# A hybrid decoder step on one core: rows gathered in their own order, early up weights in halves, the new tokens' residual in quarters

## The chip, the cores and the metric

The kernel runs on one core of one Trainium2 chip. The metric is device time in microseconds of one launch; a time that is compared is a median over several runs. One further execution was recorded by the hardware profiler, and every duration below comes from that one.

The engines are named as in the profile: PE (matmuls) with PEld (its weight loads), DVE (vector), ACT (scalar), POOL (GpSimd) and SP, whose queue issues nearly all loads of weights. Each engine works through its own instructions in their order and waits at semaphores.

## The reference

One step of one decoder layer in fp32, for 256 prompt tokens and 8 new tokens (one each for 8 sequences with 1024 past tokens in a paged cache):

```python
xn = rmsnorm(x, g_mix);  q, k, v, b, c, h = split(xn @ w_in)      # 1024 -> 6 x 512
att  = moba_attend(rope(q), [past k, rope(k)], [past v, v])      # top-3 blocks of 256 and the own block
conv = b * short_conv(c * h)
hres = x + concat(att, conv) @ w_out                             # the residual
hn   = rmsnorm(hres, g_ffn)
# router: group = argmax of 4, then the top 2 of that group's 8 experts, in fp32
h = silu(hn @ w_gate[e]) * (hn @ w_up[e]) * gate[e]              # 32 experts, 1024 -> 256
y = hres + sum_e h @ w_down[e];   y = rmsnorm(y, g_final)
```

Only the experts that a token chose count for it, so the kernel sends to each expert just its own tokens, 32 places each. The weights of the 32 experts are 96 MiB and are each read once.

## The kernel before, in words

**Tokens.** `yres[128, 3, 1024]` is the residual: t=0 and t=1 are the prompt's tokens, t=2 holds the 8 new tokens in partitions 0 to 7. `NR` = (128, 128, 8) are the tokens of each t.

**First stage.** Everything up to the router is cut into named steps, and the string `ORDER` says in which order they are issued; each engine keeps that order among its own instructions. Those that matter here: `o{t}{n}{kk}` the output projection (L779) and its add to `yres`, with `o111` and `o112` the two halves of the last; `z{n}` the output projection of the new tokens, made as four partial products that lie in the four quarters of 32 partitions, and `y{n}` the sum of these quarters (`sum_quarters`, L268) and its add to `yres` (`out_sum`, L800: four adds on 8 partitions for each half of 512 columns); `H{t}{k}` the square sum, transposes (`pt`) and scaled copy `xh` of the residual; `l{t}{k}` the router's matmuls (L878); `R`, `L`, `ra` to `re` the norm's factor and the routing of each t on DVE; `rk` and `oh` the rank of a token among its expert's and the one-hot map `Pg` from tokens to places; `hl0` the split of a residual into `hn` (rounded to fp32r, L853) and `hlo` (what is left, L868).

**Gathering.** For a group of four experts, `gather_mm` multiplies the one-hot map with the residual rows (`px`, in two halves `hf` of 512 columns), `gather_rows` copies `px` out of PSUM to `xr`, and `gather_T` transposes `xr` into `xg`, the stationary operand of the experts' matmuls. Group 0 uses `yres` itself in fp32 (L1035; each such matmul is two records of the profile), groups 1 to 7 use `hn` and `hlo` in fp32r. The expert weights lie in memory so that partition p of a weight tile holds rows 8p to 8p+7, so column 8p+c of a token has to come to partition p of chunk c. Before the change this reordering is done where `px` reads its moving operand (every eighth column for group 0) and where `hn` and `hlo` are written. In `ORDER` the gather of group 0 is `g{t}{hf}`, `ga{hf}` and `gt{hf}`.

**Experts.** A loop over eight groups `grp`: the gate matmuls `pgt` (`mm_exp`, L1205; the first matmul of each of the four experts waits for its weights), the combination of the group before (`combine_all`: `pz`, L1236, and six adds to `yres`), maps and gate values, the up matmuls `pup`, the product `sh`, its transposes `pht`, the gather of the next group, the down matmuls `pyy` (L1219) and their scaling to `Y` (`gated`). In the last group, `LAST` = 7, come also the matmuls that start the final sum from `yres` (`before`, `pzl`, L1247) and twelve matmuls that only keep PE occupied (`warm`), and the down weights and the end are cut into pieces.

**Buffers and loads.** A pool has a number of equal buffers, and a new tile takes one that is released; what first writes the tile waits for the last reader of the one before. `c4` has 10 buffers of 4 KB a partition (`xn`, `qT`, `kT`, `vn`, `kn`, `uT`, `pn`, `pT`, `Pp`, `xh`, `xr`, `xg`, `hn`, `hlo`, `Y`, and the halves `uh`), `c2` has 9 of 2 KB (among them `yq`, `Pg` and the quarters `uq`). Weights of the experts go round a ring of 15 slots of 1 MiB: two `c9`, nine `rk` (which held the cache's keys and values) and four `rw` (which held input and output projection weights). SP issues, in this order: `g0` (four gate tiles of group 0), `d0`, `g10` and `g11`, then the up weights of group 0, which have no slot of the ring but `c4` and `c2` buffers (experts 0, 1, 3 in two halves each, expert 2 in four quarters), then `g12`, `g13`, `u1`, `d1` and so on. With 15 slots, `u13` and `d10` to `d12` take the slots of `g0`, and `d13` and `g20` to `g22` those of `d0`. For group 7 the up weights come in halves and the down weights in twelve pieces.

Of the kernel before, what the change touches and what calls it, by code (L numbers as in the profile page):

```python
# [11 lines left out]
F32 = mybir.dt.float32  # L12
# [4 lines left out]
OP = mybir.AluOpType  # L17
# [24 lines left out]
cv2 b3 B10 b2 V3 cv0 V0 c2 c3 ov V2 V1 B13 eB1 G25 o010 kvs pe0 o000 eB3 G26 eB0 G27 G28 G29 o110 G30 V5 eB2 V4  # L42
o001 V6 H00 G31 o011 V7 H01 l00 pa pe o100 R0 l01 L0 ra0 rb0 rc0 o101 as co room1 rd0 re0 z0 z1 rk0 oh0 y0
y1 H10 H20 H21 l20 R2 l21 L2 ra2 rb2 room2 o111 rc2 rd2 l10 o112 H11 R1p H12a R1 H12b rk2 oh2 l11 l12 L1 ra1 rb1 rc1
g00 g01 rsa g20 rk1p rk1 oh1 g21 g10 ga0 g11 gt0 ga1 rsb gt1 rd1 sl re2 re1 hl0
"""


C_ROPE, C_SEL, C_IOTA, C_W4, C_W8, C_WT, C_HEAD, C_TOK, C_W = 0, 96, 104, 136, 140, 148, 152, 160, 172


def _table():
    t = np.zeros((128, C_W), np.float32)
    p = np.arange(128)
    inv = np.float32(500000.0) ** (-np.arange(0, 16, 2, dtype=np.float32) / np.float32(16))
    for i in range(3):
        pos = (p + 128 * i if i < 2 else np.full(128, 1024)).astype(np.float32)
        ang = pos[:, None] * inv[None, :].astype(np.float32)
        c, s = np.cos(ang), np.sin(ang)
        t[:, C_ROPE + 32 * i:C_ROPE + 32 * i + 32] = np.concatenate([c, c, -s, s], 1)  # L60
    t[:, C_SEL:C_SEL + 8] = (p[:, None] % 32) == np.arange(8)
# [27 lines left out]
def hymba_step(ctx: ExitStack, tc: tile.TileContext, x_prompt, x_sample, cache_k, cache_v, state_conv,  # L89
# [35 lines left out]
    with tc.manual_schedule():  # L125
# [139 lines left out]
        def sum_quarters(acc, x):  # L265

            for j in range(4):
                T.matmul(acc[32 * j:32 * j + 8, 0:128], lhsT=sel8, rhs=x[:, 128 * j:128 * j + 128], start=True, stop=True,  # L268
                         tile_position=(0, 32 * j))

# [524 lines left out]
        def out_sum(n):  # L795
            po2 = ps("py2", "acc")
            sum_quarters(po2, yq[n])
            for j in range(4):
                yv = yres[0:8, 2, 512 * n + 128 * j:512 * n + 128 * j + 128]
                V.tensor_tensor(yv, yv, po2[32 * j:32 * j + 8, 0:128], op=OP.add)  # L800

# [43 lines left out]
        def norm2_hi(t, a, w):  # L845
            n, p = NR[t], slice(a // 8, (a + w) // 8)
            if a == 0:
                hn[t] = c4(f"hn{t}", [128, 8, 128], F32R)
# [4 lines left out]
            S.copy(hn[t][:n, :, p].rearrange("t c p -> t p c"),  # L853
                   yres[:n, t, a:a + w].rearrange("t (p c) -> t p c", c=8))

# [7 lines left out]
        def norm2_lo(t, a, w):  # L863

            n, p = NR[t], slice(a // 8, (a + w) // 8)
            if t not in hlo:
                hlo[t] = c4(f"hlo{t}", [128, 8, 128], F32R)
            V.tensor_tensor(  # L868
                hlo[t][:n, :, p], yres[:n, t, a:a + w].rearrange("t (p c) -> t c p", c=8),
                hn[t][:n, :, p].bitcast(F32), op=OP.subtract)  # L870

# [155 lines left out]
        def gather_mm(grp, hf, tiles):  # L1027
# [5 lines left out]
            for t in tiles:  # L1033
                if grp == 0:
                    T.matmul(PX[grp, hf], lhsT=fl(PgS[grp], t, 128).bitcast(F32),  # L1035
                             rhs=yres[:, t, :].rearrange("t (p c) -> t c p", c=8)[:, 4 * hf:4 * hf + 4, :],
                             start=t == first, stop=t == last)
                    continue
                n = 40 if t == 2 else 128
                lows = (0,) if t == 2 else (0, 1)  # L1040
                for low in lows:
                    T.matmul(PX[grp, hf], lhsT=fl(PgS[grp], t, n),  # L1042
                             rhs=(hn, hlo)[low][t][:n, 4 * hf:4 * hf + 4, :].rearrange("t c p -> t (c p)"),
                             start=t == first and low == 0, stop=t == last and low == lows[-1])

        XR = {}

        def gather_rows(grp, hf):
            if hf == 0:
                XR[grp] = c4("xr", [128, 8, 128])  # L1050
            rows_, px = XR[grp][:, 4 * hf:4 * hf + 4, :].rearrange("s c p -> s (c p)"), PX.pop((grp, hf))
            w = 256 if grp == 0 else 512
            S.copy(rows_[:, 0:w], px[:, 0:w])  # L1053
# [66 lines left out]


        SPLIT = {}

        @step("room1")
        def _():
            for j in (0, 1, 3):
                SPLIT[0, "u", j] = [c4("uh", [128, 1024]) for _ in range(2)]

        @step("room2")
        def _():  # L1130
            SPLIT[0, "u", 2] = [c2("uq", [128, 512]) for _ in range(4)]

        def load_split(grp, nm, j, lst, view):
            ts = lst[grp, j] = SPLIT[grp, nm, j]
            w = 2048 // len(ts)
            for i, t in enumerate(ts):
                SP.dma_start(t, view[4 * grp + j][:, w * i:w * i + w])

        for name in ORDER.split():
            steps.pop(name)()  # L1140
        assert not steps, steps
# [12 lines left out]

        for grp in range(NE // 4):
            for lst, view, nm in ((gw, wg_v, "g"), (uw, wu_v, "u"), (dw, wd_v, "d")):
                for j in range(4):
                    if (grp, nm, j) == (1, "g", 2):
                        for k in (0, 1, 3, 2):
                            load_split(0, "u", k, uw, wu_v)  # L1160
                    if (grp, nm, j) in SPLIT:
                        continue
                    lst[grp, j] = ring(f"{nm}{grp}{j}", next(it))
                    if grp < LAST or nm == "g":
                        SP.dma_start(lst[grp, j], view[4 * grp + j])
        for a, b in ((0, 1024), (1024, 2048)):
# [106 lines left out]
        for grp in range(NE // 4):  # L1273
# [24 lines left out]
            if grp == 0:  # L1298
                slot_maps(grp)
            elif grp < LAST:  # L1300
                gather_x(grp + 1)
# [88 lines left out]
    with tc.If(flag > CAP):  # L1390
        hnT2 = c9("hnT2")
        V.memset(hnT2[:, :, 264:288], 0.0)
        for t in range(3):
            n = NR[t]
            hs = c4("hs", [128, 8, 128])
            V.tensor_tensor(hs[:n], hn[t][:n].bitcast(F32), hlo[t][:n].bitcast(F32), op=OP.add)
            V.tensor_scalar(hs[:n], hs[:n], rs2[t][:n], None, op0=OP.mult)
            for hf in range(2):
                pt = ps("pt")
                pv_ = pt.rearrange("p (c n) -> p c n", c=4)  # L1400
                for c in range(4):
                    T.transpose(pv_[:, c, 0:n], hs[:n, 4 * hf + c, :], ident[:n, :n])
                V.tensor_tensor(hnT2[:, 4 * hf:4 * hf + 4, 128 * t:128 * t + n], pv_[:, :, 0:n],
# [81 lines left out]
```

## Time and profile before

| | us |
|---|---|
| median of 3 runs (lowest, highest) | 429.58 (429.26, 432.44) |
| the profiled execution | 428.75 |
| its span, from the first to the last instruction | 426.7 |
| busy: PE, PEld, DVE, ACT, POOL | 379.3, 208.8, 198.6, 94.0, 101.6 |
| read from HBM | 152.41 MB, 362 GB/s over the span |

How to read it: durations and places come from the profiled execution, whose own time is 0.8 us under the median of the runs; a change of the span is carried over to the median as it is. PE counts as busy whenever a matmul is recorded in flight, so its 89% is no measure of how much faster it could be. A matmul's own duration contains its way through the array; where several follow each other, the distance between their starts is their cost. The granted clock is 1.00 at full speed. A row of the timeline or the chain begins with its start and its length; `xN` is a number of instructions.

### The profile page before, as it was taken

The numbers are of one execution on the slowest core, as the hardware profiler recorded it, in microseconds if no ns is written. First come the engines' busy times: TensorE is split into PE (matmuls) and PEld (weight loads), VectorE is DVE, ScalarE is ACT, GpSimd is POOL, SyncE is SP. The second block draws the span as 40 slices with busy tenths as digits, with TensorE's granted clock in tenths as the row PEclk, the third lists the DMA queues.
The fourth block names the chain that finished last, engine by engine and source line by source line (L and its number), as shares of the span: only waits on it lengthen the run. The fifth ranks groups of instructions, "written<-read, shape, count | busy, mean of one in ns | idle before, by whom it ended". The sixth has DMA issues, their size and how long they took to land.

```text
span 426.7 us, 6625 instructions
## 1 busy us (share of the span) xinstructions
PE 379.3 (89%) x2646; PEld 208.8 (49%) x2646; DVE 198.6 (47%) x389; ACT 94.0 (22%) x240; POOL 101.6 (24%) x99
## 2 busy tenths in 40 slices
PE   7999997999999999898999999996986987969971
PEld 6354354668775335363555455642533543524530
DVE  2257986899672014671763242430430431332045
ACT  4221314274330000311640111110020130110033
POOL 2727888978306000000200000000000000000031
PEclk9999999999999999988899899996996996997997
DMA  7999987879988999949899999999999999999903
GB/s 258 395 360 416 382 340 259 326 218 413 419 335 312 422 419 423 414 150 384 323 422 424 421 419 420 422 420 422 421 419 423 419 419 422 422 416 404 322 5 104
DMA packets 33125, 155.05 MB, mean 363 GB/s; under 512 B 3084, under 2 KB 5338, under 8 KB 18244
## 3 DMA queue, kind: packets, MB, share of 16 engines
q1 hardware_dynamic: 27472, 119.70, 70.3%
q0 software_dynamic: 5008, 33.80, 20.1%
q10 hardware_dynamic: 612, 1.11, 0.7%
q8 instruction: 22, 0.36, 0.3%
q14 instruction: 11, 0.09, 0.1%
HBM read 152.41 MB, written 2.20 MB: 362 GB/s over the span
## 4 chain that ended last, share of the span: by engine, by line
PE 58%; DMA 23%; DVE 9%; issue 4%; POOL 3%; ACT 1%; SPq 1%; DVEq 0%; ACTq 0%; POOLq 0%
DMA u<-in_w_up_dram 12%; DMA g<-in_w_gate_dram 9%; PE py L779 7%; PE pgt L1205 6%; PE pup L1205 5%; PE pyy L1219 4%; PE pz L1236 4%; PE px L1042 4%; PE pov L724 3%; PE acck L242 3%; PE accB L561 3%; DVE Sd L489 3%; PE accv L242 2%; PE accq L242 2%; DMA yres<-in_x_sample_dram 2%
## 5 line engine op out<-in xcount | busy, mean ns | idle before, releaser
L1205 PE MATMUL pgt<-g,xg 128*32 128x256 f32 x512 | 47.6, 481 | 18.0 <-DMA g<-in_w_gate_dram 17.7
L1270 DVE TENSOR_TENSOR yres<-yres,pz 128x512 f32<-128x512 f32 (+1 forms) x42 | 25.7, 672 | 53.6 <-PE pz L1236 53.6
L1176 POOL TENSOR_TENSOR PGw<-Pg,G 128x384 f32<-128x384 f32 x8 | 6.7, 843 | 171.6 <-PE pgs L1181 88.1
L1205 PEld LDWEIGHTS pgt<-g,xg 128*32 128x32 f32 x512 | 21.0, 137 | 45.7 <-DMA g<-in_w_gate_dram 24.0
L483 POOL TENSOR_TENSOR K<-K,qv 128x2048 f32<-128x2048 f32 x9 | 40.7, 4538 | 5.3 <-DMA K<-in_cache_k_dram,idx 3.1
L489 DVE TENSOR_REDUCE Sd<-K 128x32 f32<-128x2048 f32 x16 | 35.9, 2276 | 5.9 <-POOL K L483 5.9
L1219 PE MATMUL pyy<-d,hT 128*32 128x512 f32 (+1 forms) x272 | 32.1, 591 | 0.6 <-DVE hT L1318 0.6
L779 PE MATMUL py<-wo,mixT 128*128 128x512 f32 (+1 forms) x72 | 29.1, 552 | 0.0
L1205 PE MATMUL pup<-u,xg 128*32 128x256 f32 x448 | 25.6, 380 | 0.0
L1236 PE MATMUL pz<-Y,PT 128*128 128x512 f32 (+1 forms) x90 | 23.1, 405 | 0.0
L1228 DVE SCALAR_TENSOR_TENSOR Y<-pyy,gsl,Y 128x512 fp32r<-128x512 f32 (+1 forms) x17 | 12.1, 719 | 23.6 <-ACT Y L1227 23.6
L1296 DVE SCALAR_TENSOR_TENSOR sh<-pup,rsl,sh 128x256 f32<-128x256 f32 x8 | 5.4, 670 | 34.1 <-PE pup L1205 26.5
L1227 ACT ACTIVATE Y<-pyy,gsl 128x512 fp32r<-128x512 f32 (+1 forms) x17 | 11.2, 660 | 45.2 <-PE pyy L1219 45.1
L315 POOL DMA_INDIRECT V<-in_cache_v_dram,idx x16 | 15.6, 974 | 22.2 <-PE pov L724 18.2
L1053 ACT COPY xr<-px 128x512 f32<-128x512 f32 (+1 forms) x16 | 8.9, 559 | 50.7 <-PE px L1042 38.6
L779 PEld LDWEIGHTS py<-wo,mixT 128*128 128x128 f32 x72 | 13.2, 190 | 12.6 <-issue 12.1
L1042 PE MATMUL px<-hn,Pg 128*128 128x512 f32 (+1 forms) x42 | 19.2, 480 | 0.0
L315 POOL DMA_INDIRECT K<-in_cache_k_dram,idx x16 | 15.5, 971 | 14.7 <-DMA K<-in_cache_k_dram,idx 7.9
L1205 PEld LDWEIGHTS pup<-u,xg 128*32 128x32 f32 x448 | 13.8, 110 | 8.6
L1236 PEld LDWEIGHTS pz<-Y,PT 128*128 128x128 f32 (+1 forms) x90 | 13.2, 155 | 9.7 <-issue 2.9
L1219 PEld LDWEIGHTS pyy<-d,hT 128*32 128x32 f32 x272 | 8.8, 112 | 17.9 <-issue 16.0
L485 DVE TENSOR_TENSOR K<-K,qb 128x2048 f32<-128x2048 f32 x7 | 16.0, 2280 | 2.3 <-DMA K<-in_cache_k_dram,idx 2.3
(333 smaller groups left out, 607.1 us busy)
## 6 DMA issues: line engine op xcount, KB each, us to landing
g<-in_w_gate_dram SPq DMA_DIRECT2D x32, 1024.0 KB, 19.8
d<-in_w_down_dram SPq DMA_DIRECT2D x28, 1024.0 KB, 17.5
u<-in_w_up_dram SPq DMA_DIRECT2D x24, 1024.0 KB, 19.9
wo<-in_w_out_dram SPq DMA_DIRECT2D x4, 1024.0 KB, 16.9
u<-in_w_up_dram SPq DMA_DIRECT2D x8, 512.0 KB, 12.1
uh<-in_w_up_dram SPq DMA_DIRECT2D x6, 512.0 KB, 11.8
wk<-in_w_in_dram SPq DMA_DIRECT2D x2, 1024.0 KB, 14.4
wv<-in_w_in_dram SPq DMA_DIRECT2D x2, 1024.0 KB
```

The lines of the kernel that those rows point to most:

```text
L242: T.matmul(acc, lhsT=xnT[:, cc, 128 * t:128 * t + 128], rhs=W[pn, kk][:, c, :], start=cc == 0, stop=cc == 7)
L315: P.indirect_dma_start(out=t, out_offset=None, in_=src, in_offset=bass.IndirectOffsetOnAxis(ap=idx[:, b, hh:hh + 1], axis=0))
L483: P.tensor_tensor(kslots[i], kslots[i], qv[:, None, :].to_broadcast([128, 4, 512]), op=OP.mult)
L485: V.tensor_tensor(kslots[i], kslots[i], qbs[b][:, None, :].to_broadcast([128, 4, 512]), op=OP.mult)
L489: V.tensor_reduce(Sd[:, b, 4 * hh:4 * hh + 4, :].rearrange("p i h -> p (i h)"), kslots[i].rearrange("p i (h d) -> p (i h) d", h=8), axis=A ...
L561: T.matmul(acc[:, 0:264], lhsT=W[pn, kk][:, c, 128 * m:128 * m + 128], rhs=xnT[:, cc, 0:264], start=cc == 0, stop=cc == 7)
L779: T.matmul(po[:, lo:lo + w], lhsT=mixT[:, c, 128 * t:128 * t + 128], rhs=wo[n, c // 4][:, c % 4, lo:lo + w], start=c == 0, stop=c == 7, sk ...
L1042: T.matmul(PX[grp, hf], lhsT=fl(PgS[grp], t, n), rhs=(hn, hlo)[low][t][:n, 4 * hf:4 * hf + 4, :].rearrange("t c p -> t (c p)"), start=t == ...
L1205: T.matmul(dst[32 * j:32 * j + 32, 0:256], lhsT=xg[:, c, 32 * j:32 * j + 32], rhs=w[:, 256 * k:256 * k + 256], start=c == 0, stop=c == 7, ...
L1219: T.matmul(py[32 * j:32 * j + 32, 0:w], lhsT=hT[:, c, 32 * j:32 * j + 32], rhs=dw[grp, j][:, 1024 * c + a:1024 * c + b], start=c == 0, sto ...
L1236: T.matmul(pz, lhsT=PTS[grp][:, 128 * t:128 * t + NR[t]], rhs=Y[:, i, 0:w], start=start and i == 0, stop=i == 1, skip_group_check=more)
L1270: V.tensor_tensor(yv, yv, pz[:m], op=OP.add)
```

## The change

Five things, with the parts that go with them:

1. **The reordering moves to the eviction.** `px` reads plain halves of `yres`, `hn` and `hlo`, which are now in the tokens' own column order, and `gather_rows` writes `xr` in steps of 512 bytes. Each half of `px` now holds 64 of the 128 partitions of every chunk, so both halves must be copied before the first transpose; in `ORDER`, `gt0` stands behind `ga1`, and `g20 g21` stand ahead of the rank of t=1.
2. **The new tokens' residual is kept in quarters.** A tile `y2q[128, 2, 128]` gets `x_sample` in four small loads on POOL's queue (`xq`), one for each quarter of the partitions; the sum of the quarters now fills 32 partitions (`sel32`), one add per half goes to all quarters, and the square sum and one transpose per half start from there. A matmul over the partitions (`pss`) adds the square sums, and four copies on ACT (`yr`) bring the result to `yres`. `H20 H21` go ahead of `H10`.
3. **Up weights of group 0** are eight halves in `c4`, allotted and issued at step `room1`, right behind the step `ld0` that issues `g0`, `d0`, `g10` and `g11`. The order on SP stays.
4. **`hl0` is gone from the first stage.** `hn` of t=0 and t=1 are made behind `pup` of group 0, `hlo` behind its gate values.
5. **`combine_all(6)`** stands at the end of group 6, ahead of group 7's gate matmuls.

```diff
-y1 H10 H20 H21 l20 R2 l21 L2 ra2 rb2 room2 o111 rc2 rd2 l10 o112 ...
-g00 g01 rsa g20 rk1p rk1 oh1 g21 g10 ga0 g11 gt0 ga1 rsb gt1 rd1 sl re2 re1 hl0
+... H00 G31 o011 V7 xq H01 ... as co ld0 room1 rd0 re0 z0 z1 rk0 oh0 y0
+y1 H20 H21 H10 yr l20 l21 R2 L2 ra2 rb2 o111 rc2 rd2 l10 o112 ...
+g00 g01 g20 g21 rk1p rk1 oh1 rsa g10 ga0 g11 ga1 rsb gt0 gt1 rd1 sl re2 re1
...
 def out_sum(n):
     sum_quarters(po2, yq[n])
+    V.tensor_tensor(Y2["q"][:, n, :], Y2["q"][:, n, :], po2[:, 0:128], op=OP.add)
-    for j in range(4):
-        yv = yres[0:8, 2, 512 * n + 128 * j:512 * n + 128 * j + 128]
-        V.tensor_tensor(yv, yv, po2[32 * j:32 * j + 8, 0:128], op=OP.add)
+@step("xq")
+    Y2["q"] = c2("y2q", [128, 2, 128])
+    P.memset(Y2["q"], 0.0)
+    for j in range(4):
+        P.dma_start(Y2["q"][32 * j:32 * j + 8], xv[j])
+@step("yr")
+    for j in range(4):
+        S.copy(yv[:, :, j, :], Y2["q"][32 * j:32 * j + 8])
...
 def norm2_half(t, k):
+    if t == 2:
+        y = Y2["q"][:, k, :]
+        S.activation(sqj[:, 0:128], y, AF.Square, accum_out=ss2[t][:, k:k + 1])
+        T.transpose(pt[:, 0:128], y, ident)
 def norm2_hi(t, a, w):
-    S.copy(hn[t][:n, :, p].rearrange("t c p -> t p c"), yres[:n, t, a:a + w].rearrange("t (p c) -> t p c", c=8))
+    S.copy(hn[t][:n, a:a + w], yres[:n, t, a:a + w])
 def norm2_lo(t, a, w):
+    V.tensor_tensor(hlo[t][:n, a:a + w], yres[:n, t, a:a + w], hn[t][:n, a:a + w].bitcast(F32), op=OP.subtract)
 def norm2_pre(t):
+    if t == 2:
+        T.matmul(pss[0:8, 0:2], lhsT=sel8, rhs=ss2[t][:, 0:2], start=True, stop=True)
 def gather_mm(grp, hf, tiles):
-    rhs=yres[:, t, :].rearrange("t (p c) -> t c p", c=8)[:, 4 * hf:4 * hf + 4, :],
+    rhs=yres[:, t, 512 * hf:512 * hf + 512],
 def gather_rows(grp, hf):
-    rows_, px = XR[grp][:, 4 * hf:4 * hf + 4, :].rearrange("s c p -> s (c p)"), PX.pop((grp, hf))
+    rows_ = XR[grp][:, :, 64 * hf:64 * hf + 64].rearrange("s c p -> s p c")
+    px = PX.pop((grp, hf)).rearrange("s (p c) -> s p c", c=8)
...
+@step("ld0")
+    load(0, "g", range(4)); load(0, "d", range(4)); load(1, "g", (0, 1))
 @step("room1")
+    for j in range(4):
+        uw[0, j] = [c4("uh", [128, 1024]) for _ in range(2)]
+        for i, t in enumerate(uw[0, j]):
+            SP.dma_start(t, wu_v[j][:, 1024 * i:1024 * i + 1024])
...
 for grp in range(NE // 4):
     if grp:
-        combine_all(grp - 1, Ys)
+        if grp < LAST:
+            combine_all(grp - 1, Ys)
...
     Ys = [gated(grp, down(grp, hT, 512 * n, 512 * n + 512), 512) for n in range(2)]
+    if grp == LAST - 1:
+        combine_all(grp, Ys)
```

The constant table grows from 172 to 196 columns for `sel32`.

More of the change, by code (lines that the diff above doesn't have):

```diff
@@ L42 @@
 cv2 b3 B10 b2 V3 cv0 V0 c2 c3 ov V2 V1 B13 eB1 G25 o010 kvs pe0 o000 eB3 G26 eB0 G27 G28 G29 o110 G30 V5 eB2 V4
[L43 to L45 removed]
+o001 V6 H00 G31 o011 V7 xq H01 l00 pa pe o100 R0 l01 L0 ra0 rb0 rc0 o101 as co ld0 room1 rd0 re0 z0 z1 rk0 oh0 y0
+y1 H20 H21 H10 yr l20 l21 R2 L2 ra2 rb2 o111 rc2 rd2 l10 o112 H11 R1p H12a R1 H12b rk2 oh2 l11 l12 L1 ra1 rb1 rc1
+g00 g01 g20 g21 rk1p rk1 oh1 rsa g10 ga0 g11 ga1 rsb gt0 gt1 rd1 sl re2 re1
 """
[L49 removed]
+C_ROPE, C_SEL, C_IOTA, C_W4, C_W8, C_WT, C_HEAD, C_TOK, C_W = 0, 96, 128, 160, 164, 172, 176, 184, 196
 def _table():
@@ L267, in sum_quarters @@
             for j in range(4):
-                T.matmul(acc[32 * j:32 * j + 8, 0:128], lhsT=sel8, rhs=x[:, 128 * j:128 * j + 128], start=True, stop=True,
-                         tile_position=(0, 32 * j))
+                T.matmul(acc[32 * j:32 * j + 32, 0:128], lhsT=sel32, rhs=x[:, 128 * j:128 * j + 128], start=True,
+                         stop=True, tile_position=(0, 32 * j))
         def samp_sum(pn):
@@ L845, in norm2_hi @@
         def norm2_hi(t, a, w):
[L846 removed]
+            n = NR[t]
             if a == 0:
[L848 removed]
+                hn[t] = c4(f"hn{t}", [128, D], F32R)
                 if t == 2:
@@ L863, in norm2_lo @@
         def norm2_lo(t, a, w):
-            n, p = NR[t], slice(a // 8, (a + w) // 8)
+            n = NR[t]
             if t not in hlo:
[L867 to L870, printed above, removed]
+                hlo[t] = c4(f"hlo{t}", [128, D], F32R)
+            V.tensor_tensor(hlo[t][:n, a:a + w], yres[:n, t, a:a + w], hn[t][:n, a:a + w].bitcast(F32), op=OP.subtract)
         def norm2_log(t, k):
@@ L1119, in hymba_step @@
         steps["rsb"] = lambda: gather_rs(0, (1,))
[L1122 to L1141, printed above, removed]
         wg_v = w_gate.rearrange("o e (p c) f -> (o e) p (c f)", c=8)
@@ L1153, in ring, with load, _ @@
             return c9(name, (128, 2048)) if tag == "c9" else slot(name, tag)
-        for grp in range(NE // 4):
-            for lst, view, nm in ((gw, wg_v, "g"), (uw, wu_v, "u"), (dw, wd_v, "d")):
-                for j in range(4):
[L1158 to L1165, printed above, removed]
+        def load(grp, nm, js):
+            lst, view = {"g": (gw, wg_v), "u": (uw, wu_v), "d": (dw, wd_v)}[nm]
+            for j in js:
+                lst[grp, j] = ring(f"{nm}{grp}{j}", next(it))
+                SP.dma_start(lst[grp, j], view[4 * grp + j])
+        @step("ld0")
+        def _():
+            load(0, "g", range(4))
+            load(0, "d", range(4))
+            load(1, "g", (0, 1))
+        @step("room1")
+        def _():
+            for j in range(4):
+                uw[0, j] = [c4("uh", [128, 1024]) for _ in range(2)]
+                for i, t in enumerate(uw[0, j]):
+                    SP.dma_start(t, wu_v[j][:, 1024 * i:1024 * i + 1024])
+        for name in ORDER.split():
+            steps.pop(name)()
+        assert not steps, steps
+        load(1, "g", (2, 3))
+        load(1, "u", range(4))
+        load(1, "d", range(4))
+        for grp in range(2, LAST):
+            for nm in "gud":
+                load(grp, nm, range(4))
+        load(LAST, "g", range(4))
+        for j in range(4):
+            uw[LAST, j] = ring(f"u{LAST}{j}", next(it))
+        for j in range(4):
+            dw[LAST, j] = ring(f"d{LAST}{j}", next(it))
         for a, b in ((0, 1024), (1024, 2048)):
@@ L1299, in hymba_step @@
                 slot_maps(grp)
+                for t in (0, 1):
+                    for a in (0, 512):
+                        norm2_hi(t, a, 512)
             elif grp < LAST:
@@ L1325, in hymba_step @@
                 slot_gates(grp)
-                norm2_lo(1, 0, 512)
-                norm2_lo(1, 512, 512)
+                for t in (0, 1):
+                    for a in (0, 512):
+                        norm2_lo(t, a, 512)
                 norm2_both(2)
@@ L1401, in hymba_step @@
                 for c in range(4):
-                    T.transpose(pv_[:, c, 0:n], hs[:n, 4 * hf + c, :], ident[:n, :n])
+                    T.transpose(pv_[:, c, 0:n], hs.rearrange("t (p c) -> t c p", c=8)[:n, 4 * hf + c, :], ident[:n, :n])
                 V.tensor_tensor(hnT2[:, 4 * hf:4 * hf + 4, 128 * t:128 * t + n], pv_[:, :, 0:n],
```

30 lines of the change are left out of this document (16 added, 14 removed).

## Prediction, before the changed kernel ran

> **What bounds the kernel now.** I read the slices of the page first, then a table of stretches, then the chain that ended last.
>
> ```profile
> GB/s 258 395 360 416 382 340 259 326 218 413 419 335 312 422 419 423 414 150 384 323 422 424 421 419 420 422 420 422 421 419 423 419 419 422 422 416 404 322 5 104
> ```
>
> A slice is a fortieth of the span, 10.67 us. The loads are over by slice 38 (405.4 us); the last dent before the plateau of 420 GB/s is slices 17 to 19. Finer (columns: stretch, its length, busy time of the five engines, then granted clock, DMA share, GB/s):
>
> ```profile
> 166.00:182.00 16.00, 14.05 (x110) 7.32 (x109) 9.77 (x47) 4.20 (x12) 0.54 (x1) 1.00 1.01 416
> 182.00:188.00 6.00, 5.46 (x35) 4.60 (x34) 4.93 (x26) 1.30 (x7) 0.61 (x2) 1.00 0.28 111
> 188.00:194.00 6.00, 6.00 (x10) 2.27 (x9) 2.57 (x13) 0.00 (x0) 0.00 (x0) 0.58 0.74 186
> 194.00:207.00 13.00, 11.66 (x64) 4.66 (x66) 4.96 (x27) 4.39 (x13) 0.00 (x0) 0.80 1.02 423
> 207.00:210.00 3.00, 3.00 (x64) 1.68 (x56) 2.77 (x4) 2.80 (x5) 0.72 (x1) 1.00 0.44 115
> 230.00:385.00 155.00, 133.31 (x1188) 71.66 (x1188) 46.01 (x76) 22.70 (x49) 4.99 (x6) 0.92 1.01 420
> ```
>
> From 230 to 385 us the transfers never pause. Below 420 GB/s, 182 to 188 loses 6 x 309/420 = 4.4 us, 188 to 194 loses 6 x 234/420 = 3.3, and 207 to 210 loses 3 x 305/420 = 2.2: 9.9 us in all. Who held the queue of SP, 160 to 215 us:
>
> ```profile
> SPq L1165 <- PE pgt L1205: 12.8, 1, 12.8
> SPq L1137 <- DVE xh L842: 6.0, 1, 6.0
> 180.82 7.37 SPq L1137 DMA_DIRECT2D uh<-in_w_up_dram  x2
> ```
>
> Two halves of group 0's up weights went out at 180.82 and 187.87, each within 0.1 us of the router matmuls L878 that last read an `xh` (they end at 180.74 and 187.85 in the chain below). The wait for `pgt` is the second: `u13` and the three `d1` behind it take the slots of `g0`, free when group 0's gate matmuls end. In the chain (start, us, what) the first rows are that stage, the others the end:
>
> ```profile
> 159.53 1.85 PE pov L724 x16
> 180.03 0.71 PE pl L878 x16
> 180.74 1.93 PE py L779 x8
> 187.20 0.65 PE pl L878 x4
> 203.41 4.90 PE pgt L1205 x64
> 208.31 3.53 PE pup L1205 x64
> 217.32 3.11 PE px L1042 x10
> 245.90 3.45 PE pgt L1205 x64
> 266.87 3.45 PE pgt L1205 x64
> 365.02 19.97 DMA g<-in_w_gate_dram
> 385.03 6.26 PE pgt L1205 x58
> 391.29 3.00 PE pz L1236 x12
> 401.89 3.63 PE pup L1205 x64
> 407.37 2.77 PE pyy L1219 x24
> ```
>
> So there are three links: a PE and DVE chain to the end of `pgt` of group 0 (208.31); then a stream at full rate until `g7` lands (385.03); then 41.7 us of PE work that waits for no load. The end moves by (shift of the stream) + (what the tail loses).
>
> **The change, part by part.** All of it against the profiled execution, 428.75 us with a span of 426.7.
>
> *Quarters.*
>
> ```profile
> L800 DVE TENSOR_TENSOR yres<-yres,py x8: 269/280/289, 176.4 to 178.6; 8x128 f32<-8x128 f32 x8
> 185.12 0.21 ACT L980 ACTIVATE rcols<-rcols 128x4 f32<-128x4 f32 x1 [5.46 <-DVE rcols L978]
> 165.10 0.58 POOL L899 TENSOR_TENSOR rsb<-rs,mhalf 128x1 f32<-128x1 f32 x1 [27.86 <-DVE rs L898]
> ```
>
> Eight adds fill 176.5 to 178.85 while PE waits for the last of them; after an `xh` of t=1 and one transpose come `l20` and `l21` at 180.03 (0.71) and `o111` at 180.74. After the change there are two adds of 0.28. I put the second, which waits for the second sum's matmuls, at 177.0 to 177.3; one transpose (0.3), a short `xh` (0.2) and the 0.71 give 178.5, with 0.2 for semaphores 178.7: **-2.0 us**. Bounds: -2.3 (all adds but two and `xh` gone) and -1.0 if the new sum over partitions (`pss`, one matmul of about 0.25) and the later `xh` of t=1 cost DVE time there. The copies `yr` (four, between 0.25 for an 8x128 and 0.6 for a 512-wide copy, some 1.6) lie on ACT, which sits idle for the 5.46 us before 185.12; without that cover they would hold up `route`'s exponentials by up to 1.6. The load `xq` (a memset and four DMAs) stands on POOL behind the last V gather, in the 27.86 idle us before 165.10, and is due at 176.5. Both at nothing.
>
> *Rows in their own order.* Six matmuls each, L1035 with steps of 32 bytes, L1247 reading the same `yres` contiguously:
>
> ```profile
> 194.54 5.84 PE L1035 MATMUL px<-yres,Pg 128*128 128x512 f32 x6
> 396.08 2.93 PE L1247 MATMUL pzl<-yres,ident 128*128 128x512 f32 x6
> 190.70 0.25 DVE L969 SCALAR_TENSOR_TENSOR A<-rcols 128x32 bf16<-128x32 f32 x1
> 189.00:194.00 5.00, 5.00 (x9) 2.06 (x8) 1.71 (x9) 0.00 (x0) 0.00 (x0) 0.50 0.85 216
> ```
>
> Without the tail of the last one that is 0.92 us against 0.43 a record (each matmul has two). The first six records, from 187.67 on and partly at clock 0.50, have the same spacing, so the read sets it and not the clock. On the path, in old times: `g00 g01 g20 g21` take 8 x 0.43 from 187.67, to 191.1; `A` of t=1 is there at 190.95, so rank, `rka` and `Pg` (1.0 by estimate: three short instructions like that row, and their semaphores) give 192.15; `g10 g11` 4 x 0.43 end at 193.9, against 194.54 + 5.84 = 200.38 now. **-6.5 us** at full clock. At half clock a record would take 0.86 and nearly all of it is gone. [...] For those writes the nearest rows are `hn`, written at the same step of 512 bytes, and the contiguous cast and subtraction of the same shape:
>
> ```profile
> L853 ACT CAST hn<-yres x6: 1101/1158/1169, 206.2 to 214.8; 128x512 fp32r<-128x512 f32 x4, 8x512 fp32r<-8x512 f32 x2
> L461 ACT CAST qhi<-partq x1: 618/618/618, 21.8 to 21.8; 128x512 fp32r<-128x512 f32 x1
> L868 DVE TENSOR_TENSOR hlo<-yres,hn x4: 1099/1120/1151, 207.4 to 214.5; 128x512 fp32r<-128x512 f32 x4
> L462 DVE TENSOR_TENSOR qlo<-partq,qhi x1: 692/692/692, 22.5 to 22.5; 128x512 fp32r<-128x512 f32 x1
> L1053 ACT COPY xr<-px x16: 372/585/587, 198.6 to 372.7; 128x512 f32<-128x512 f32 x14, 128x256 f32<-128x256 f32 x2
> ```
>
> Reading PSUM with such a write isn't in the trace: between 0.585 and 1.16 for 512 columns; I take 1.1. For group 0, `ga1` starts 0.25 after 193.9, ACT 0.6 and then DVE 0.6 (each 256 columns), both halves before `gt0`; transposes and `xg` 1.1 more: `pgt` at 196.5, that is 2.6 after the last `px` against 3.03 now: **-0.4**, between -0.6 and +0.6. In groups 1 to 7 `gather_T` waits for both copies: about +1.0 us of PE a group. That is hidden: `pgt` of groups 2 and 3 start 266.87 - 245.90 = 21 us apart, and the 12 MiB of a group take 30 at 420 GB/s. Without that cover it would cost 7 us.
>
> *hn, hlo* of t=0 and t=1 now run between `pup` and `pyy` of group 0: ACT 4 x 0.62, DVE 4 x 0.69, and t=2 2 x 0.69: 4.15 on DVE, against the 4 x 1.1 there now. `px` (217.32) isn't later.
>
> `pgt` of group 0 thus starts at 203.41 - 2.0 - 6.5 - 0.4 = 194.5 and, at the half clock of today (4.90; the row is among the rivals), ends 8.9 us earlier, at 199.4.
>
> *Up weights.* SP's order is the old one; only the buffers change. At `room1` the ten `c4` buffers are free but for readers that end by then; taken in the order in which they were released, the eight halves get ones last read by `pov` (159.53 + 1.85 = 161.4) at the latest, where two of the old six got those of `xh`. SP itself isn't moved past any queue: the same transfers follow each other on it. The quarters go. So the 4.4 and the 3.3 us should close. The stretches from 166 to 207 moved 416x16 + 111x6 + 186x6 + 423x13 = 13.94 MB, which at 420 GB/s are done at 199.2. `u13` is then freed at 199.4 and its bytes flow some 1 us later: a gap of 1 to 1.5 us where 9.9 were. **Stream: -8.6 us.** Bounds: -9.9 (no gap) and -3.7 (the first rival).
>
> After that, releases keep ahead: the batch freed by `pgt` is 4 MiB, 10 us of loading; `pyy` of group 0 frees the next at 217.32, 9.0 us after `pgt`. The margin is 1 to 2 us and grows by 9 a group.
>
> *combine_all(6) ahead of pgt(7).* It goes from the tail into the wait for `g7`: `pz` 391.29 to 394.28, **-3.0 us**, if `pup` finds its weights.
>
> ```profile
> L1168 SPq DMA_DIRECT2D u<-in_w_up_dram x8: 327/328/328, 367.5 to 385.0; - x8
> DMA to landing us min/median/max: 10.2/12.1/14.0
> 386.33 14.88 SPq L1172 DMA_DIRECT2D d<-in_w_down_dram  x12
> ```
>
> The last `u7` lands by 385.0 + 14.0 = 399, 2.9 us ahead of `pup` at 401.89; both move with the stream but `pup` 3.0 more, so they may just touch, and only the second half of `pup` (1.8 us in) reads it. All `d7` pieces, issued after it, are in by 405.4; the first third of them, which `pyy` reads first, is wanted at 407.37 - 3.0, relative to the stream. Bounds: -3.0 and -2.0. `pgt` of group 7 runs at half clock today (6.26 against 3.45 for 64 at full); with `pz` in the pause it may keep the clock: 0 to -2.7, I take -0.4.
>
> Sum: -8.6 - 3.0 - 0.4 = **-12.0 us**. The runs shown have median 429.58, 0.8 above the profiled one: **417.6**.
>
> **Rivals.** *The clock halves the gathers.*
>
> ```profile
> 203.00:206.00 3.00, 3.00 (x30) 1.27 (x33) 2.34 (x17) 2.08 (x6) 0.00 (x0) 0.50 1.03 434
> ```
>
> For: the clock was 1.00 to 188 and 0.50 from 189 to 194, after a stretch of transposes and 36-column matmuls, and 0.50 again under `pgt`; that stretch stays. Against: from 166 to 182 it held 1.00 with PE idle for 2 of 16 us, and dense reads keep PE busier than the stepped ones. If all 12 records run at 0.86, 12 x 0.43 = 5.2 of the 8.9 are lost; the stream restarts 3.7 earlier: -3.7 - 3.0 - 0.4 = -7.1, **422.5**. [...]
>
> *The stage is freed but the buffers aren't* (the change doesn't do what it says): if two halves still get buffers of `xh`, freed 2.0 us earlier than now, some 3.4 of the 4.4 us stay, and then nothing waits for `pgt`: the stream gains 6.5, total -9.9, **419.7**. For: it is so today; against: the count above.
>
> *The tail waits for loads:* `pz` gains nothing, -9.0, **420.6**. Against: 2.9 us of margin.
>
> *Slower: the strided eviction.* Two a group sit between `px` and `pgt`. From 0.585 + 9/2 = 5.1 us each PE, not the stream, would set a group; to eat the 12 us over seven groups takes 1.7 us a group more, 6.0 us each; at 8 us each it is 7 x 2 x 2.9 - 12 = +29, **458**. Its nearest row has 1.16.
>
> **How the numbers follow.** Forecast 0.58 (414 to 420), halved gathers 0.20 (420 to 424), buffers 0.08, tail 0.06, slower 0.03, and 0.05 that several small losses leave it within 1%. Those 0.05 and a little of the rivals give same 0.06; faster 0.91, slower 0.03; 1% (4.3 us) is about what runs of this kernel can tell. The lower end takes all gains at their bounds, -9.9 - 3.0 - 2.7 = -15.6, 414.0; the upper reaches past the halved gathers: 423.5.
>
> **What would show it.** Right: 420 GB/s from 166 to about 199, no row of SP waiting for `xh`; `px` of group 0 at 0.43 spacing; `pgt` of group 0 at 194 to 196; `g7` landing at 376; `pz` before it. Wrong: clock 0.50 during `px`, `xr` copies far above 1.1 us, or a pause of the stream between 200 and 240 because `pyy` of group 0 is late.

## The result, and the profile after

| | before | after |
|---|---|---|
| median of four runs, us | 431.01 | 413.49 |
| lowest, highest | 429.26, 433.26 | 412.54, 413.86 |
| profiled execution (span) | 428.75 (426.7) | 413.36 (411.7) |

The ratio is 0.9587, 95% interval 0.953 to 0.9644: faster, and 4.1 us more so than the 417.6 forecast. Between the two profiled executions the gain is 15.4 us where the sum had 12.0; the last 0.7 us is the distance from the profiled execution to the median, 0.8 before and 0.1 after.

The page of the changed kernel, GB/s by slices of 10.3 us:

```profile
span 411.7 us, 6612 instructions
GB/s 278 398 373 410 373 368 223 322 301 297 419 406 262 406 414 415 420 413 421 404 420 417 420 419 422 423 420 420 422 419 421 419 421 423 420 419 410 382 122 111
```

Behind the thirteenth value (262, the stage before the loads of experts begin) there is no dent any more. The same stretches as before (length, five engines, granted clock, DMA share, GB/s):

```profile
182.00:188.00 6.00, 5.48 (x28) 3.69 (x27) 5.00 (x26) 1.30 (x7) 0.62 (x2) 1.00 1.04 419
188.00:194.00 6.00, 4.72 (x21) 2.64 (x20) 2.57 (x9) 1.19 (x3) 0.00 (x0) 1.00 1.02 424
194.00:207.00 13.00, 12.59 (x178) 6.79 (x176) 8.69 (x32) 7.50 (x19) 2.81 (x3) 1.00 1.00 407
207.00:210.00 3.00, 3.00 (x13) 1.53 (x9) 1.85 (x3) 1.69 (x2) 0.00 (x0) 1.00 1.03 415
```

111, 186 and 115 GB/s have become 419, 424 and 415, and the clock stays at 1.00 where it was 0.58 and 0.80. PE on its way to the first gate matmuls, and SP's queue over the same time (start, us, what):

```profile
185.76 3.68 PE L1056 MATMUL px<-yres,Pg 128*128 128x512 f32 x8
190.30 1.98 PE L1056 MATMUL px<-yres,Pg 128*128 128x512 f32 x4
193.59 1.09 PE L1099 MATMUL pxt<-ident,xr 128*128 128x128 f32 x8 [1.19 <-DVE xr L1078]
194.76 3.66 PE L1230 MATMUL pgt<-g,xg 128*32 128x256 f32 x64
```

```profile
166.32 13.24 SPq L1173 DMA_DIRECT2D uh<-in_w_up_dram  x8
183.63 15.13 SPq L1159 DMA_DIRECT2D u<-in_w_up_dram  x4
198.85 8.90 SPq L1159 DMA_DIRECT2D d<-in_w_down_dram  x4
```

The eight halves go out between 166 and 180. Three of the four `u1` follow. The last one waits for `pgt` of group 0 (us in all, times, longest):

```profile
SPq L1159 <- PE pgt L1230: 11.6, 1, 11.6
```

It ends its issue at 198.8, when `pgt` is done (194.76 + 3.66 = 198.4; 203.41 + 4.90 = 208.3 before). So the gate matmuls still release the stream, 9.9 us earlier and just as the loads issued ahead of them run out. The tail, in the chain that ended last:

```profile
355.48 19.84 DMA g<-in_w_gate_dram
375.37 3.64 PE pgt L1230 x58
379.00 0.52 PE ppt L1217 x3
379.53 0.84 PE pgs L1206 x6
380.37 2.86 PE pzl L1272 x6
383.24 2.88 PE warm L298 x24
386.11 3.63 PE pup L1230 x64
404.93 1.86 DVE yres L1415 x3
```

`g7` is used from 375.37 on, 9.66 earlier. From there to the last copies (`yres`, 404.93; 420.72 before) it is 29.56 us against 35.69, 6.13 less: `pz` is gone (3.0), `pgt` takes 3.64 instead of 6.26 (2.62), and `pgs` no longer waits for ACT's copy behind `ppt` (0.5). The end behind these copies, the last write of the output, is 0.8 longer. -9.66 - 6.13 + 0.79 = -15.0, the difference of the spans. From the start of these copies to the end of the span it takes between 5.2 and 7.3 us in the seventeen profiles, whatever was changed, so the 0.8 is scatter, and two single spans can't be compared closer than that.

### The profile page after: what moved, and what is told of

It is laid out like the page before. It is cut to its first block, busy times and chain, and to the rows that moved or that the text cites. A ratio compares the mean times of both kernels' runs of the same rounds, so it can differ in the third digit from the quotient of the medians.

```text
span 411.7 us, 6612 instructions
## 1 busy us (share of the span) xinstructions
PE 369.4 (90%) x2642; PEld 207.7 (50%) x2642; DVE 194.0 (47%) x383; ACT 98.0 (24%) x244; POOL 103.9 (25%) x104
## 5 line engine op out<-in xcount | busy, mean ns | idle before, releaser
L1230 PE MATMUL pgt<-g,xg 128*32 128x256 f32 x512 | 42.2, 451 | 16.4 <-DMA g<-in_w_gate_dram 16.0
L1230 PEld LDWEIGHTS pgt<-g,xg 128*32 128x32 f32 x512 | 19.8, 129 | 39.5 <-DMA g<-in_w_gate_dram 21.1
L1076 ACT COPY xr<-px 128x512 f32<-128x512 f32 (+1 forms) x16 | 15.7, 982 | 43.1 <-PE px L1063 36.1
L1303 ACT ACTIVATE sh<-pgt,rsl 128x256 f32<-128x256 f32 x8 | 3.8, 475 | 55.0 <-PE pgt L1230 55.0
```

The lines of the kernel that those rows point to most:

```text
L1230: T.matmul(dst[32 * j:32 * j + 32, 0:256], lhsT=xg[:, c, 32 * j:32 * j + 32], rhs=w[:, 256 * k:256 * k + 256], start=c == 0, stop=c == 7, ...
```

## The experiments

Times are medians in us, of four to six runs (ten for one kernel). The kernel before had medians between 430.2 and 431.4 in the same sets of runs, the changed kernel 413.49.

**The stream: which part brought the loads forward?** Three undo one thing in the changed kernel, two more separate what the first ones left mixed, and one does a part alone.

```diff
 a_stepped_reads, group 0 alone
-    rhs=yres[:, t, 512 * hf:512 * hf + 512]
+    rhs=yres[:, t, :].rearrange("t (p c) -> t c p", c=8)[:, 4 * hf:4 * hf + 4, :]
     (and its eviction writes contiguously)
```

> The changed kernel, but the gather of group 0 reads the residual in steps of 32 bytes again and writes its rows contiguously; everything else stays. Theory (the end of the gate matmuls of group 0 releases the stream, so what the gather loses the whole kernel loses): twelve records at 0.92 us instead of 0.43 and the one-hot map of t=1 behind the first eight give +6.0 on the path, the eviction -0.4, and if the granted clock falls to 0.50 again another +1.2 in the gate matmuls: 413.5 + 5.6 to 6.8 = 419.1 to 420.3. Rival (the new buffers of the up weights alone brought the stream forward): 413.5 to 414.5. On the clock: if the stepped reads are what lowers it, 0.50 shows between 186 and 200 us; if the transposes ahead of them are, it stays at 1.00 as in the changed kernel.

Measured 419.06 (ratio to before 0.9735, 0.9672 to 0.9797), at the lower end of what the theory gave and far from the rival: the theory stands.

```profile
185.75 7.58 PE L1056 MATMUL px<-yres,Pg 128*128 128x512 f32 x8
194.20 3.92 PE L1056 MATMUL px<-yres,Pg 128*128 128x512 f32 x4
198.14 1.34 PE L1104 MATMUL pxt<-ident,xr 128*128 128x128 f32 x8
199.41 0.85 PE L1235 MATMUL pgt<-g,xg 128*32 128x256 f32 x12
```

The records are back at 0.93 us and `pgt` starts 4.65 us later (the last row is cut at 200 us). The reads end 5.8 later (198.1 against 192.3), but the transposes start at once behind them: the first four need only the first half of `xr`, which is copied by then. In the changed kernel each half holds a part of every chunk, and the transposes wait 1.19 for both. The `g7` of this profile is used 4.56 later than in the changed kernel; the other 0.6 between the two spans is the last write. The clock fell, to 0.51 over each of the stretches from 187.8 to 191.2 and from 194.6 to 198.0.

```diff
 a_no_quarters
-    V.tensor_tensor(Y2["q"][:, n, :], Y2["q"][:, n, :], po2[:, 0:128], op=OP.add)
+    for j in range(4):   # eight adds on 8 partitions, as before
+        V.tensor_tensor(yv_j, yv_j, po2[32 * j:32 * j + 8, 0:128], op=OP.add)
 a_no_quarters_warm, besides: nine idle matmuls behind H10
```

> The changed kernel, but the new tokens' residual on 8 partitions as before: eight adds, no quarters, no matmul over the partitions. Theory: the path to the gate matmuls of group 0 is 2.0 us longer and the stream that much later, 415.5 (with the clock unchanged; 416.7 if the gate matmuls fall to half clock). Rival (this stage ends before the loads that it would release can flow): 413.5.

> The changed kernel with the new tokens' residual on 8 partitions again (eight adds) and nine matmuls that only keep PE occupied (2.2 us) ahead of the transposes that wait for these adds. Theory (of the 3.8 us that this undo cost without them, 2.0 are the longer path and the rest the clock that fell in the wait): clock 1.00 from 166 to 210 us, gate matmuls of group 0 at about 196.8 us, and 415.5, with less scatter than the 414.8 to 419.5 without them. Rival (the whole 3.8 is the path): 417.3.

Measured 417.26 (0.966, 0.9594 to 0.9726) without the idle matmuls and 414.21 (0.9622, 0.9581 to 0.9664) with them, the first with a scatter from 414.81 to 419.49. The first was beyond its forecast. Its profile is of the slowest of its four executions, and has the clock down from 178.7 to 185.5 us, behind the wait for the adds:

```profile
175.20:178.60 3.40, 2.04 (x29) 1.11 (x25) 2.81 (x11) 2.03 (x6) 0.00 (x0) 1.00 1.00 410
178.60:182.00 3.40, 2.82 (x23) 2.50 (x24) 1.90 (x10) 0.62 (x2) 0.55 (x1) 0.51 1.02 407
```

With the wait filled the second stretch reads 1.00:

```profile
178.60:182.00 3.40, 3.31 (x36) 2.81 (x35) 1.94 (x10) 0.57 (x2) 0.55 (x1) 1.00 1.04 413
```

and `pgt` starts at 196.42:

```profile
196.42 3.66 PE L1207 MATMUL pgt<-g,xg 128*32 128x256 f32 x64
```

That is 1.66 us behind the changed kernel's 194.76: the path of the quarters. `pgt` without the filling started at 198.86, so the other 2.4 was clock (and another 1.7 in that slow execution was `pgt` of group 7, at 5.33 instead of 3.64). The kernel with the filling missed its own forecast of 415.5 by 1.3 on the fast side, 0.7 above the changed kernel. In its profile the 1.66 arrives at the last copies as 1.61, but the last write is 1.5 shorter. So the 1.66 is shown on the path; in the time, with this scatter, it is not.

```diff
 a_old_buffers: six halves in c4 and four quarters in c2, issued behind ORDER
 a_old_buffers_split, besides
+    steps["hl0"] = lambda: norm2_both(0)      # hn, hlo of t=0 in the first stage
```

> The changed kernel, but the up weights of group 0 in six halves and four quarters as before, in the buffers that fall to them. Theory (the stream needs both: loads that don't wait for buffers, and the release by the gate matmuls): two halves wait for the router's matmuls at about 178 and 186, the stream loses between 3.6 and 6.9 us of loading and has 0.5 of slack, 416.5 to 420, likeliest 418.4. Rival (the end of the gate matmuls alone sets the stream): 413.5 to 414.5.

> The changed kernel with the up weights in six halves and four quarters as before and, besides, hn and hlo of t=0 made in the first stage again, so that two halves get buffers of the normalised residual as in the kernel before. Theory (the room came from moving hn and hlo; with the two halves waiting for the router's matmuls at about 178 and 186 us, the stream is dry from 182 on): 2.9 + 3.3 us of loading lost less 0.5 of slack, 419.2, between 416.4 and 420. Rival (these loads are hidden behind the wait for the gate matmuls anyway): 413.5 to 415.5.

The first measured 415.55 (0.9633, 0.9577 to 0.9689), and doesn't test its theory: with `hl0` gone the six halves don't get the buffers of `xh` at all, and 182 to 188 shows 406 GB/s. Its `pgt` of group 7 took 5.33 us, 1.7 more than in the changed kernel, which is most of the difference. The second measured 418.82 (0.9744, 0.9693 to 0.9794), as its theory had it, and the waits of SP show the buffers:

```profile
SPq L1188 <- DVE xh L863: 9.2, 2, 6.6
SPq L1160 <- PE pgt L1240: 5.2, 1, 5.2
```

So the room for the up weights came from moving `hl0`, not from the halves as such. Then the converse, those two edits alone on the kernel before:

```diff
 b_buffers (the kernel before)
-... sl re2 re1 hl0          # ORDER
+    eight halves at room1, right behind ld0; hn and hlo of t=0 and t=1 behind pup of group 0
```

> The kernel before with only the up weights in eight halves issued amid the first stage and with hn and hlo of t=0 moved behind it, which frees the room for them; the rows are still gathered in steps and the new tokens still on 8 partitions. Theory (the end of the gate matmuls of group 0 at 208 us releases the stream, whatever came before): the dent from 182 to 194 us closes, the loads run dry at about 199 instead and wait for 208 to 209, so the stream gains at most 0.5 to 1: 430.4, against 431.4 for the kernel before. Rival (the loads that waited for buffers were the loss): 4.4 to 7.7 gained, 424 to 427.

Measured 431.45 against 430.56 (ratio 1.0036, 1.0002 to 1.0069): nothing gained. The dent at 182 closed (419 GB/s) and opened again at 200 (the last `u1` waits 21.3 us for `pgt`, where it was 12.8):

```profile
194.00:200.00 6.00, 6.00 (x10) 1.66 (x9) 0.91 (x3) 0.37 (x1) 0.00 (x0) 0.85 0.95 395
200.00:207.00 7.00, 5.67 (x55) 2.97 (x57) 4.03 (x24) 3.36 (x11) 0.00 (x0) 0.76 0.03 9
```

Loads that don't wait are worth nothing without the earlier release, and 5.3 with it; the earlier gather is worth 5.6 beside them. The release doesn't need the loads in the same way: `a_old_buffers_split`, whose loads wait as before, is 11.4 below the kernel before (430.18), and only 5.8 of that is the combination of group 6 (`b_combine_ahead` below).

**The tail and the clock.**

```diff
 a_combine_back
-                if grp < LAST:
-                    combine_all(grp - 1, Ys)
+                combine_all(grp - 1, Ys)
-            if grp == LAST - 1:
-                combine_all(grp, Ys)
 a_combine_back_warm, besides: sixteen idle matmuls where it had stood
 b_combine_ahead: the kernel before with this one edit of the change
```

> The changed kernel, but the combination of group 6 behind the gate matmuls of group 7 again. Theory (the twelve matmuls leave the tail, and their activity shortly ahead of the gate matmuls keeps these at full clock): 3.0 + 2.6 = 5.6 us back, 419.1, with the gate matmuls of group 7 at about 6.3 us. Rival 1 (the full clock there is luck of timing): 3.0 back, 416.5, gate matmuls at 3.6. Rival 2 (the tail waits for its loads): 413.5 to 414.5.

> The changed kernel with the combination of group 6 behind the gate matmuls of group 7 again and sixteen matmuls that only keep PE occupied (3.9 us) in the place where it stood. Theory (any matmul activity ahead of the wait for the last gate weights keeps the clock): gate matmuls of group 7 at 3.6 us, and only the 3.0 us of the combination come back: 416.5. Rival (the clock there is luck of timing, or the twelve matmuls of the combination themselves matter): as with the combination merely put back, 419.3, and gate matmuls at 5 us or more.

> The kernel before with only the combination of group 6 moved ahead of the gate matmuls of group 7. Theory (it leaves the tail, and its activity keeps those gate matmuls at full clock): 3.0 + 2.6 = 5.6 less than 431.4, 425.8, with the gate matmuls at about 3.6 us. Rival (the clock there is luck of timing): 3.0 less, 428.4, and the gate matmuls at 5 to 6.3 us.

Measured 419.26 (0.9721, 0.9664 to 0.9778), 416.51 (0.9693, 0.9637 to 0.9748) and 424.77 (0.9884, 0.9819 to 0.9948, against 430.56). All three medians went by the theory: 3.0 us are the combination, and matmuls that compute nothing buy back 2.8. The last gate matmuls in the three, in this order:

```profile
376.51 5.04 PE L1230 MATMUL pgt<-g,xg 128*32 128x256 f32 x58 [1.89 <-DMA g<-in_w_gate_dram]
```

```profile
375.70 3.64 PE L1230 MATMUL pgt<-g,xg 128*32 128x256 f32 x58 [1.90 <-DMA g<-in_w_gate_dram]
```

```profile
386.18 3.64 PE L1205 MATMUL pgt<-g,xg 128*32 128x256 f32 x58 [1.88 <-DMA g<-in_w_gate_dram]
```

The clock is only part of the 2.8 in these profiles. `pgt` took 5.04 instead of 3.64, 1.4, and not the 6.3 that was forecast; of the rest, 0.8 is a `g7` that came earlier and 1.0 a shorter last write. And activity ahead isn't all of it: `a_old_buffers`, `a_no_quarters` and `a_no_warm` (below) have the combination ahead and 5.33 us. With the combination ahead and the wait left open it was 3.64 in five of eight profiles, with nothing ahead 5.02 to 6.26 in all three. Whether the remaining wait of 1.9 us is what decides was tried by filling it:

```diff
 a_fill
             if grp == LAST - 1:
                 combine_all(grp, Ys)
+                keep_warm(7)          # seven idle matmuls, 1.7 us
```

> The changed kernel with seven matmuls that only keep PE occupied (1.7 us) at the end of group 6, behind the combination, in the 1.9 us in which PE waits for the last gate weights. Theory (the clock drops for one window of 3.41 us when PE idles through most of the window before, so a filled wait leaves no drop): gate matmuls of group 7 at 3.6 us in the profile, and the same time as the changed kernel whose profiled run had the clock too, 413.5, between 412.8 and 413.8, with less scatter. Rival (the drop doesn't hang on this wait): gate matmuls at 5.3 us in some runs, scatter of 1.7 and a median of 414 to 415.

Measured 412.83, from 412.42 to 413.56 (0.9582, 0.9544 to 0.9619); `pgt` of group 7 took 3.64. The result agrees with the theory; one profile can't exclude luck.

**The cover of the slower eviction.**

```diff
 a_more_pe
                 gather_x(grp + 1)
+                keep_warm(24)         # groups 1 to 6, 5.5 us each
```

> The changed kernel with twenty-four matmuls that only keep PE occupied (5.8 us) behind the gather in each of groups 1 to 6. Theory (the loads set the pace of these groups at 30 us, PE needs 22 to 23, so the slower eviction of 1 us a group and these 5.8 are hidden): 413.5, or up to 415.2 if the gate matmuls of group 7 fall on the low clock. Rival (PE is close to the bound there): 5 to 35 us more, 418 to 448.

Measured 417.55 (0.9703, 0.9656 to 0.9751): neither. The clock was 1.00 up to the last 10 us and the loads ran at 420 GB/s in nearly all stretches, but two places had no cover for 5.5 us. The first is the start of the row of groups, where PE is behind and releases slots later; there 1.5 us of loading were lost:

```profile
228.00:249.00 21.00, 20.44 (x198) 14.19 (x202) 7.67 (x14) 3.51 (x8) 0.27 (x1) 1.00 0.96 391
```

The other is its end. In the chain PE waits for the last up weights of group 6, and from there it has 21.6 us to do up to `pgt` of group 7, which then waits for no load:

```profile
336.89 20.55 DMA u<-in_w_up_dram
357.49 3.64 PE pup L1230 x58
365.16 5.47 PE warm L298 x48
379.14 3.59 PE pgt L1230 x64
```

Without the idle matmuls that is 16.2 us, beside 19.8 us of loading (the `g` row of the changed kernel's chain above): 3.7 free at the last group, not the 9 of the middle groups. (That is at full clock; in the changed kernel's own profile PE waits 1.85 there.) The slower eviction takes 0.9 of that in each group.

**Versions meant to be better**: less PE work between `g7` and the end.

```diff
 a_no_warm:  KEEP = 0
 v_halves:   KEEP = 0, and g7 in halves of the chunks, as u7 is
 v_halves_d: besides, the first piece of d7 in two loads of 256 columns
 v_order:    besides, the combination ahead of the second piece's down matmuls
```

> The changed kernel without the twelve matmuls that only occupy PE ahead of the up matmuls of group 7 (2.9 us of the tail). Theory (with the combination gone from the tail its weights are only just in time: by the rate of the stream the last up weights land at about 386 and the first third of the down weights at about 391): 0 to 1 us gained, likeliest 413.1, with waits for the loads in the up and down matmuls. Rival (the tail after the last gate weights is PE work alone): 2.9 gained, 410.6.

> A version meant to be better: the changed kernel with the gate weights of group 7 loaded in halves of the chunks (all four first halves ahead of the second ones) and without the twelve matmuls ahead of the last up matmuls. Theory (behind the last gate weights only half of the gate matmuls is left, 1.8 us instead of 3.6, and 2.9 of occupied PE goes, but the first third of the down weights lands some 15.1 us behind the last gate weights and the down matmuls stand at 16.3 now): 1.2 gained, 412.3. Rival (the tail is PE work alone): 4.7 gained, 408.8.

> As the version in halves, and the first third of group 7's down weights comes in two loads of 256 columns with its matmuls in two sets. Theory (the down matmuls can start when the first sixth is in, some 12.7 us behind the last gate weights, and end 1.4 us behind the second): 2.4 gained, 411.1. Rival (finer loads are slower, or the pieces behind it then set the end): 412.3 or above.

> The version in halves with the first third of the down weights in two loads, and the combination of the first half ahead of the second part's down matmuls, which wait for loads. Theory (in that version these down matmuls waited for their weights and held up the combination behind them by about 0.9 us): 412.5. Rival (the last loads set the end in any order): 413.4.

Measured 414.06 (0.9628, 0.9575 to 0.9682), 413.65 (0.9635, 0.9587 to 0.9682), 413.37 (0.9606, 0.957 to 0.9643) and 412.75 (0.958, 0.9541 to 0.9618). The first three gained nothing, short of their forecasts by 1.0, 1.4 and 2.3. In the profile of `a_no_warm` the 2.9 us went into a `g7` that came 1.5 later and a `pgt` at half clock, 1.7, so it doesn't decide. `v_halves` does, and the rival that the tail is PE work alone falls: PE comes to the down matmuls 1.8 us earlier, with waits for loads on the way, and waits there again:

```profile
384.74 0.62 PE L1234 MATMUL pup<-u,xg 128*32 128x256 f32 x2 [0.55 <-DMA u<-in_w_up_dram]
386.02 1.91 PE L1234 MATMUL pup<-u,xg 128*32 128x256 f32 x26 [0.66 <-DMA u<-in_w_up_dram]
389.85 1.29 PE L1248 MATMUL pyy<-d,hT 128*32 128x512 f32 x6 [0.59 <-DVE hT L1348]
391.48 2.56 PE L1248 MATMUL pyy<-d,hT 128*32 128x512 f32 x18 [0.35 <-DMA d<-in_w_down_dram]
```

They end at 394.0, in the changed kernel at 394.4. `v_order` and `a_fill` are 0.7 us below the changed kernel's median, which overlaps with their scatter, and their ratios to before (0.958 and 0.9582) are that of the changed kernel (0.9587): not told apart.

## Why the prediction went wrong, by its own steps

**What bounds the kernel.** Right, and tested: a release by the first gate matmuls, a stream at 420 GB/s, a tail. From the end of `pgt` of group 0 to the use of the last `g7` it is 176.7 us before and 176.9 after, and 176.8 to 177.0 in `a_stepped_reads`, `a_no_quarters` and `a_no_quarters_warm`, where `pgt` ends 1.7 to 4.6 later. (In `a_combine_back` and `a_no_warm`, which don't touch this stretch, it is 178.0 and 178.6: one profile can be off by that much.) Every sign of being right that the prediction named came; the size is what it missed.

**Quarters**, -2.0 on the path: `o111` starts at 178.21 instead of 180.74, 2.5 earlier, of which 0.5 was there at 172 us already; 1.66 by `a_no_quarters_warm`. `yr` and `xq` cost nothing. What the step lacked is that the wait it removes could also cost the clock, 2.4 us in one profile.

**Rows in their own order**, -6.5: the last `px` ends 8.1 us earlier, less the 1.9 that the stage before it gave (`px` starts at 185.76, not 187.67), is 6.2. The rank was ready as priced. The eviction by 512 columns, now written in steps of 512 bytes, went from 0.585 to 1.04 (1.1 taken), 256 columns took 0.59 on both engines, and the step from the last `px` to `pgt` 2.5 instead of 3.0 (-0.5, -0.4 taken). The 1 us a group is hidden, but the cover is 3.7 us at the last group and not 9, so the slower rival would have decided at a lower price than it named.

**`hn` and `hlo`**, nothing on the path: right. That this edit was the one that freed the room was not seen; the count of free buffers at `room1` was right.

**Up weights.** The dent closed as forecast (9.9 us lost then, under 0.5 now). The stream was put at -8.6 and gave -9.66, since `pgt` of group 0 was priced at the half clock of the kernel before (4.90) and took 3.66.

**`combine_all(6)`.** -3.0 as priced, and a wait of 0.5 ahead of `pgs` that went with it. The loads of the tail were in time, as the margin of 2.9 us said; `v_halves` shows that little of it is left.

**The failing step is the clock**, twice: "at the half clock of today" for group 0's gate matmuls, worth 1.1 of the stream, and "0 to -2.7, I take -0.4" for group 7's, which gave -2.6. The text had the argument against its own value, that dense reads keep PE busier and `pz` fills the pause, and kept the old duration anyway. Part of the gain was luck: of the eight profiles with group 7's wait left open behind the combination, three have 5.33 there and not 3.64. For group 0's gate matmuls the cause stays open. They took 3.66 in all thirteen profiles with dense reads and 4.9 to 5.2 in the three that share the old first stage, but 3.66 in `a_stepped_reads` too, so the reads alone don't settle it. With -9.66, -2.62 and -3.5 in its sum, +0.8 at the end and -0.4 between span and time, it comes to the -15.4 that were measured. The rival of the halved gathers, given 0.20, happens with reads in steps (`a_stepped_reads`), and in none of the thirteen profiles with dense ones. The lower end, 414.0, took every gain at its bound and still lay 0.5 above the result, by the 0.7 between the profiled execution and the median.

## What to carry to other kernels

An edit can be worth nothing or five microseconds, depending on another at the same place: here loads that wait for no buffer gained only once a consumer released the next buffers early enough. Price a stage in which the clock dips at both clocks, and ask of each removed or added wait of some 2 us what it does to the clock behind it (0.51 behind the open wait of `a_no_quarters`, 1.00 behind the filled one). The cover of this loop was smallest in its first and last round: count it there, not from the period in the middle.

## What the hardware showed that was not expected

The granted clock takes two values, 1.00 and 0.50, and its changes lie on a grid of 3.41 us. In the kernel before it is 0.50 from 188.98 to 195.81 us and from 202.63 to 206.04, in the changed kernel from 71.12 to 74.53 and from 282.74 to 289.57: 6.83 or 3.41 us each. In `v_halves_d` one dip lasts more than 9.0, from 280.3 to beyond 289.3. In these and ten more profiles the changes inside the kernel are whole multiples of 3.41 us apart, and the grid lies elsewhere in each execution (a dip starts at 282.74 in the changed kernel and at 283.66 in `v_order`). In `a_no_warm` most of the wait for the last gate weights falls into one window, which has PE busy for 0.74 of 3.40 us, and the next one runs at half clock, 1.7 us lost:

```profile
373.60:377.00 3.40, 0.74 (x6) 0.26 (x10) 0.69 (x2) 0.00 (x0) 0.00 (x0) 1.00 1.01 407
377.00:380.40 3.40, 3.40 (x36) 1.75 (x37) 0.00 (x0) 0.00 (x0) 0.00 (x0) 0.50 1.02 407
```

In the changed kernel the same wait is cut in two by the grid, and neither window lowered the clock:

```profile
371.50:374.90 3.40, 1.92 (x11) 0.55 (x10) 3.04 (x6) 0.00 (x0) 0.00 (x0) 1.00 1.00 406
374.90:378.30 3.40, 2.94 (x56) 1.82 (x57) 0.00 (x0) 0.00 (x0) 0.00 (x0) 1.00 1.03 410
```

Ahead of the drop in `a_no_warm` PE has gaps of 1.1 and 1.9 us, 2.7 us of them in that one window. Busy time alone doesn't decide: 1.92 us of it held the clock in the changed kernel, and 2.04, half of them transposes, did not in `a_no_quarters`. What does decide was not tried.

The reads in steps of 32 bytes go with a lower clock: in all four profiled kernels that have them (the one before, `b_buffers`, `b_combine_ahead`, `a_stepped_reads`) it fell to 0.50 between 186 and 200 us, in none of the thirteen with dense reads. Three of the four share the whole old first stage; only `a_stepped_reads` has the reads alone. There the clock fell though PE was recorded busy for 3.17 of 3.40 us, rose behind a window of nothing but such reads at half clock, and fell again:

```profile
184.40:187.80 3.40, 3.17 (x15) 1.66 (x13) 2.75 (x15) 0.24 (x2) 0.62 (x2) 1.00 1.04 414
187.80:191.20 3.40, 3.40 (x5) 0.97 (x4) 1.09 (x6) 0.00 (x0) 0.00 (x0) 0.51 1.01 419
191.20:194.60 3.40, 3.31 (x11) 1.32 (x10) 0.48 (x2) 0.00 (x0) 0.00 (x0) 0.99 1.01 422
194.60:198.00 3.40, 3.40 (x6) 0.99 (x5) 0.42 (x1) 0.37 (x1) 0.00 (x0) 0.51 1.02 424
```

A record took 0.93 us in steps at both clocks and 0.43 dense at full clock, from start to start (the records themselves last 1.10 and 0.59). By these numbers such a read may leave PE waiting for half of its time at full clock and for little of it at half clock, which would fit; that is a guess and was not tried by itself.
